# Splitting the weights of a hybrid decoder layer into high and low parts: one operation per pair of K tiles, with three weight buffers

## The chip, the cores and the metric

The kernel runs on one core of a Trainium2 chip. A core has a matrix engine (PE, with its weight loads shown apart as PEld), a vector engine (DVE), a scalar engine (ACT), a fourth engine that this kernel does not use (POOL), and DMA queues that the engines issue; nearly all loads of this kernel are issued by SyncE (SP). The metric is the device time of one execution in microseconds; lower is better. The profile is of one execution of the kernel, taken apart from the timed ones.

## The reference

One decoder layer over 256 tokens of 4096 channels, in float32. The inputs are normalised, projected once to 12,288 columns, mixed in three branches, gated, normalised by branch, projected back, added to the residual and normalised again:

```python
h = rmsnorm(x, ln_g)
proj = h @ w_in                                   # 4096 x 12288
p_x, p_gate, q, k, v, a_gate, s_u, s_gate = jnp.split(proj, _SPLIT_OFFSETS, axis=-1)
y_pool = pool_mixer(p_x, w_pool, pool_scale)
y_attn = stick_breaking_attention(q, k, v)        # reshaped to 16 heads
y_ssm  = s5_mixer(s_u, ..., w_glu, b_glu)         # ends in a GLU: h @ w_glu
...                                               # per branch: rmsnorm, times silu(gate)
out = rmsnorm(x + concat(branches) @ w_out, final_g)
```

## The kernel before

**Precision.** A float32 product is made of three matmuls in a reduced format (fp32r): each operand is split into a high part, which is a rounded copy, and a low part, the operand less that copy, and the products high x high, high x low and low x high are summed in PSUM. ScalarE makes the high part (a copy with rounding), VectorE the low part (a subtraction that reads the weights and the high part).

**The stream.** All weights come as one stream of 528 steps (`N_SUB`). A step is a pair of K tiles: one weight tile `w` of 128 partitions x 2 x 512 float32, 512 KB, loaded by one DMA on SP's queue. Steps 0 to 399 are the input projection (24 units of 512 columns with 16 steps each) and four shorter GLU units of 4 steps; steps 400 to 527 are the output projection, eight "out" units of 16 steps. In the loop (L860 to L921) step i first issues the load of step i + 4 (`LOAD_AHEAD`), then splits the weights of step i + 2 (`SPLIT_AHEAD`), then issues the matmuls of step i, and then pumps a share of the side work of the three branches (scans, attention, gates, transposes).

**Forms of a step.** `mm_chan` (L241 to L247) has the weights as the stationary operand and makes 24 matmuls of 256 columns; `mm_tok` (L234 to L239) streams the weights and makes 12 matmuls of 512 columns. In each out unit the steps 2, 5, 7, 9 and 11 (`SEVEN`) are made by the seven-product scheme of Strassen and Winograd on the four 128 x 256 blocks of the weight pair, 21 matmuls of 256 columns (`mm_seven`, L169 to L185). Such a step needs three raw blocks in high and low parts (`split_seven`, L158) and four sums of blocks, also in high and low parts (`sums_seven`, L147: the differences `t7` by VectorE, then a high part of 128 x 1024 by ScalarE and a low part of 128 x 1024 by VectorE). They are joined at the unit's end (`join_seven`, L187).

**What sets the order.** SP's queue is issued in the order in which the code is written. The order on the other engines is made by a scheduler when the program is built, which knows the operations and their dependences; each engine then runs its queue strictly in that order. A tile from a pool with n buffers waits until the last reader of the tile n allocations earlier is done. So a load of `w` waits for the low part of the pair whose buffer it takes, and a high part waits for the matmuls that read the buffer that it takes.

**Names and lines.** `load_first` L125 (step 0, loaded as two halves with the first pieces of x between them), `load` L135, `hi_lo` L140, `split` L210 (high part at L228, low part through the helper at L82), `split_x` (the activations, ACT at L94 and DVE at L91), `constants` L717 (four small loads at the start of unit 1, i.e. step 16; three pass through one staging tile `raw`), `square_x` (sums of squares of x, one piece `xsq` of 512 KB at eight of the steps from 16 on), `load_out` L759 (residual `xr` and norm weights `fg` at step 7 of each out unit). In the last four steps the matmuls of the second token half are held back to the tail (L927 to L947), so their split weights stay in tiles of their own (`held8`, `held4`).

Of the kernel before, what the change touches and what calls it, by code (L numbers as in the profile page):

```python
# [23 lines left out]
NU = 512  # L24
# [5 lines left out]
LOAD_AHEAD = 4  # L30
SPLIT_AHEAD = 2
HELD = 4
# [20 lines left out]
N_SUB = 24 * 16 + 4 * 4 + 8 * 16  # L53


def body(tc, a, out, ctx):
# [20 lines left out]
    bp = pool("base")  # L77
# [3 lines left out]
    def tt(o, x, y, op):  # L81
        V.tensor_tensor(o, x, y, op)  # L82
# [10 lines left out]
    def act(o, x, f, **kw):  # L93
        S.activation(o, x, f, **kw)  # L94
# [25 lines left out]

# [1 line left out]
    wtiles, htiles = {}, {}  # L122
    held = []

    def load_first():  # L125
        w = wp.tile([P, 2, NU], F32, tag="w", bufs=LOAD_AHEAD, name="w")
        xt = bp.tile([P, 2, L], F32, tag="k4", bufs=6, name="xt")
        for j in range(2):
            nc.sync.dma_start(w[:, j, :], a["ws"][0, :, j, :])
            if j == 0:  # L130
                nc.sync.dma_start(prm, a["prm"])
            nc.sync.dma_start(xt[:, j, :], a["xT"][0, :, j, :])
        wtiles[0], xtiles[0] = w, xt

    def load(i):  # L135
        w = wp.tile([P, 2, NU], F32, tag="w", bufs=LOAD_AHEAD, name="w")
# [10 lines left out]
    def sums_seven(i):  # L147
        w = wtiles[i]
        left, right = w[:, :, 0:L], w[:, :, L:2 * L]
        t = bp.tile([P, 4, L], F32, tag="k4", bufs=6, name="t7")  # L150
        tt(t[:, 0:2, :], right, w[:, 0, :].rearrange("p (c m) -> p c m", c=2), ALU.subtract)
        tt(t[:, 2, :], right[:, 1, :], t[:, 0, :], ALU.subtract)
        tt(t[:, 3, :], left[:, 1, :], t[:, 2, :], ALU.subtract)
        sums = bp.tile([P, 2, 4, L], F32R, tag="k8", bufs=3, name="sums7")
        hi_lo(sums[:, 0], sums[:, 1], t)
        htiles[i] = sums

    def split_seven(i):  # L158
# [8 lines left out]
        htiles[i] = (raw, htiles[i])  # L167

    def mm_seven(i, s, ps, pp):  # L169
        (b11, b2), sums = htiles.pop(i)  # L170
# [4 lines left out]
        for o, stat, mov, begin, end in (  # L175
            (pp[0], xa[:, :, lo_half], [v[:, 0:L] for v in b11], first, last),
            (ps[:, 0, 0:L], xb[:, :, lo_half], [v[:, 0:L] for v in b2], False, False),
            (ps[:, 0, L:2 * L], y[:, 2], [v[:, L:2 * L] for v in b2], False, False),
            (pp[1], y[:, 0], [sums[:, h, 0] for h in range(2)], False, last),
            (pp[3], xa[:, :, hi_half], [sums[:, h, 1] for h in range(2)], first, last),  # L180
            (pp[2], y[:, 1], [sums[:, h, 2] for h in range(2)], False, last),
            (ps[:, 1, 0:L], xb[:, :, hi_half], [sums[:, h, 3] for h in range(2)], False, False),
        ):
            for k, (p, q) in enumerate(((0, 0), (0, 1), (1, 0))):
                T.matmul(o, stat[:, p, :], mov[q], start=begin and k == 0, stop=end and k == 2, skip_group_check=True)  # L185

    def join_seven(pp, xr):  # L187
        e = bp.tile([P, 4, L], F32, tag="k4", bufs=6, name="e7")
        act(e[:, 0, :], pp[0], AF.Copy)
        tt(e[:, 3, :], e[:, 0, :], pp[2], ALU.add)  # L190
        tt(e[:, 1, :], e[:, 3, :], pp[1], ALU.add)
        tt(e[:, 2, :], e[:, 3, :], pp[3], ALU.add)
        tt(e[:, 3, :], e[:, 2, :], pp[1], ALU.add)
        tt(xr, xr, e.rearrange("p (t c) m -> p t (c m)", t=2), ALU.add)
# [15 lines left out]
    def split(i):  # L210
        if seven(i):
            return split_seven(i)
        w = wtiles.pop(i)
        for kk in range(2):
            if i < KT // 2:
                split_x(2 * i + kk)
            h = 2 * (i - N_SUB + HELD) + kk
            if h < 0:
                hi = wp.tile([P, NU], F32R, tag="hi", bufs=5, name="hi")
                lo = wp.tile([P, NU], F32R, tag="lo", bufs=5, name="lo")  # L220
            elif h < 6:
                if h % 2 == 0:
                    held.append(bp.tile([P, 2, 2, NU], F32R, tag="k8", bufs=3, name="held8"))
                hi, lo = held[-1][:, kk, 0, :], held[-1][:, kk, 1, :]
            else:
                held.append(bp.tile([P, 2, NU], F32R, tag="k4", bufs=6, name="held4"))
                hi, lo = held[-1][:, 0, :], held[-1][:, 1, :]
            made = S.activation(hi, w[:, kk, :], AF.Copy)  # L228
            if i == 12:
                state["gate"] = made.ins.name  # L230
            tt(lo, w[:, kk, :], hi.bitcast(F32), ALU.subtract)
            htiles[i, kk] = (hi, lo)

# [14 lines left out]

# [1 line left out]
    state = {}  # L250
# [28 lines left out]

# [1 line left out]
    def log1pexp_parts(z, l):  # L281
# [47 lines left out]

# [1 line left out]
    pool_sums = cp.tile([P, 2, 2], F32, name="pool_sums")  # L331
# [43 lines left out]

# [1 line left out]
    uT = bp.tile([P, 8, L], F32, tag="k8", bufs=3, name="uT")  # L377
# [206 lines left out]

# [1 line left out]
    aout = {}  # L586
# [66 lines left out]

# [1 line left out]
    cur = {}  # L655
# [31 lines left out]

# [1 line left out]
    units = []  # L689
# [351 lines left out]
```

## Time and profile before

| what | value |
|---|---|
| time, median of 3 runs (lowest, highest) | 1558.77 us (1558.5, 1559.57) |
| profiled execution, span from first to last instruction | 1556.4 us |
| the runs' median less that span | 2.4 us |
| mean granted clock of PE | 0.998 |
| data moved by DMA | 308.45 MB, mean 198 GB/s |
| first matmul starts, last one ends | 5.27 us, 1545.4 us |

The profiled execution's time is taken as its span and what lies around it. The page of a profile lists the busy time of each engine, the span in slices, the chain of work that ended last, and the costliest groups of instructions: line, engine, operation, `out<-in` by the program's names with its shape, the count, busy us, mean ns of one, the idle time of the engine just before them, and what ended most of that. Engines other than the bound one have idle time that costs nothing.

### The profile page before, as it was taken

The numbers are of one execution on the slowest core, as the hardware profiler recorded it, in microseconds if no ns is written. First come the engines' busy times: TensorE is split into PE (matmuls) and PEld (weight loads), VectorE is DVE, ScalarE is ACT, GpSimd is POOL, SyncE is SP. The second block draws the span as 40 slices with busy tenths as digits, with TensorE's granted clock in tenths as the row PEclk, the third lists the DMA queues.
The fourth block names the chain that finished last, engine by engine and source line by source line (L and its number), as shares of the span: only waits on it lengthen the run. The fifth ranks groups of instructions, "written<-read, shape, count | busy, mean of one in ns | idle before, by whom it ended". The sixth has DMA issues, their size and how long they took to land.

```text
span 1556.4 us, 25428 instructions
## 1 busy us (share of the span) xinstructions
PE 1538.2 (99%) x9164; PEld 1360.9 (87%) x9164; DVE 1201.6 (77%) x2325; ACT 913.9 (59%) x1637; POOL 0.2 (0%) x4
## 2 busy tenths in 40 slices
PE   8999999999999999999999999999999999999996
PEld 8998788888799989998998889988888888888885
DVE  7579978999898879897556745455678888888886
ACT  7655556666565555565546754456667655555554
POOL 0000000000000000000000000000000000000000
PEclk9999999999999999999999999999999999999999
DMA  8866656566655546554555555545556666666665
GB/s 320 306 214 205 195 162 205 186 206 194 205 188 185 187 156 197 176 175 162 183 186 180 180 185 183 183 159 186 190 178 193 212 220 220 216 214 210 204 222 198
DMA packets 94079, 308.45 MB, mean 198 GB/s; under 512 B 11777, under 2 KB 17665, under 8 KB 93953
## 3 DMA queue, kind: packets, MB, share of 16 engines
q1 hardware_dynamic: 84096, 296.08, 58.2%
q10 hardware_dynamic: 9856, 10.76, 2.3%
q8 instruction: 71, 1.16, 0.3%
q14 instruction: 56, 0.45, 0.1%
HBM read 299.45 MB, written 4.19 MB: 195 GB/s over the span
## 4 chain that ended last, share of the span: by engine, by line
PE 96%; DVE 2%; DMA 1%; ACT 1%; issue 0%; SPq 0%; DVEq 0%; ACTq 0%
PE pm L238 18%; PE pm L237 18%; PE pm L239 18%; PE pm L245 10%; PE pm L247 10%; PE pm L246 10%; PE ps L185 3%; PE pm L185 3%; DVE lo L82 1%; PE ps_y L572 1%; DMA w<-in_ws 1%; PE ps_bu L545 0%; ACT hi L228 0%; PE ps_z L598 0%; PE ps_p L356 0%; PE ps_t L296 0%
## 5 line engine op out<-in xcount | busy, mean ns | idle before, releaser
L82 DVE TENSOR_TENSOR lo<-w,hi 128x512 fp32r<-128x512 f32 (+1 forms) x1048 | 696.9, 678 | 273.1 <-ACT hi L228 266.0
L228 ACT ACTIVATE hi<-w 128x512 fp32r<-128x512 f32 x968 | 604.6, 629 | 503.2 <-PE pm L239 204.4
L238 PE MATMUL pm<-lo,xhl 128*128 128x512 f32 x1232 | 482.4, 392 | 0.0
L239 PE MATMUL pm<-hi,xhl 128*128 128x512 f32 x1232 | 480.8, 390 | 0.0
L237 PE MATMUL pm<-hi,xhl 128*128 128x512 f32 x1232 | 480.6, 390 | 0.0
L245 PE MATMUL pm<-xhl,hi 128*128 128x256 f32 x1280 | 363.8, 284 | 5.3 <-ACT xhl L94 5.3
L246 PE MATMUL pm<-xhl,hi 128*128 128x256 f32 x1280 | 363.5, 284 | 0.0
L247 PE MATMUL pm<-xhl,lo 128*128 128x256 f32 x1280 | 363.4, 284 | 0.0
L238 PEld LDWEIGHTS pm<-lo,xhl 128*128 128x128 f32 x1232 | 231.5, 188 | 48.9 <-issue 2.1
L239 PEld LDWEIGHTS pm<-hi,xhl 128*128 128x128 f32 x1232 | 231.4, 188 | 47.3 <-issue 1.2
L237 PEld LDWEIGHTS pm<-hi,xhl 128*128 128x128 f32 x1232 | 231.5, 188 | 46.9 <-issue 0.4
L245 PEld LDWEIGHTS pm<-xhl,hi 128*128 128x128 f32 x1280 | 246.6, 193 | 7.1 <-ACT xhl L94 5.3
L247 PEld LDWEIGHTS pm<-xhl,lo 128*128 128x128 f32 x1280 | 246.6, 193 | 1.2 <-issue 0.8
L246 PEld LDWEIGHTS pm<-xhl,hi 128*128 128x128 f32 x1280 | 246.6, 193 | 0.8 <-issue 0.4
L91 DVE SCALAR_TENSOR_TENSOR et<-et,pw,tr 128x16 f32<-128x16 f32 (+3 forms) x256 | 55.6, 275 | 2.3 <-ACT tr L94 1.9
L94 ACT ACTIVATE sums<-t 128x1024 fp32r<-128x1024 f32 x40 | 42.3, 1058 | 23.8 <-DVE t L82 23.3
L82 DVE TENSOR_TENSOR sums<-t,sums 128x1024 fp32r<-128x1024 f32 x40 | 48.9, 1223 | 8.8 <-ACT sums L94 8.7
L94 ACT ACTIVATE hi<-w 128x256 fp32r<-128x256 f32 x80 | 40.0, 518 | 22.4 <-PE pm L239 18.9
L185 PE MATMUL ps<-sums,s 128*128 128x256 f32 x240 | 46.5, 283 | 1.1 <-DVE sums L82 1.1
L94 ACT ACTIVATE tr<-et,pw 128x32 f32<-128x32 f32 (+3 forms) x128 | 44.7, 384 | 4.7 <-DVE et L91 2.0
L82 DVE TENSOR_TENSOR t<-w 128x512 f32<-128x512 f32 x40 | 27.6, 690 | 24.3 <-DMA w<-in_ws 24.0
L560 DVE TENSOR_TENSOR_SCAN tb<-rho,ta 128x256 f32<-128x256 f32 x64 | 40.6, 676 | 0.1
(258 smaller groups left out, 1261.3 us busy)
## 6 DMA issues: line engine op xcount, KB each, us to landing
w<-in_ws SPq DMA_DIRECT2D x527, 512.0 KB, 3.5
xsq<-in_xr SPq DMA_DIRECT2D x8, 512.0 KB, 7.2
xr<-in_xr SPq DMA_DIRECT2D x8, 512.0 KB, 4.5
out<-o SPq DMA_DIRECT2D x8, 512.0 KB, 4.0
xt<-in_xT SPq DMA_DIRECT2D x15, 256.0 KB, 6.1
b<-in_bst ACTq DMA_DIRECT2D x16, 192.0 KB, 3.6
u<-uT ACTq DMA_DIRECT2D x96, 32.0 KB, 3.0
fg<-in_fg SPq DMA_DIRECT2D x8, 256.0 KB, 5.9
```

The source lines that it names most:

```text
L82: V.tensor_tensor(o, x, y, op)
L91: V.scalar_tensor_tensor(o, x, s, y, op0, op1)
L94: S.activation(o, x, f, **kw)
L185: T.matmul(o, stat[:, p, :], mov[q], start=begin and k == 0, stop=end and k == 2, skip_group_check=True)
L228: made = S.activation(hi, w[:, kk, :], AF.Copy)
L237: T.matmul(ps[t], stat[:, slot, 0, sl], hi, start=first, stop=False)
L238: T.matmul(ps[t], stat[:, slot, 0, sl], lo, start=False, stop=False)
L239: T.matmul(ps[t], stat[:, slot, 1, sl], hi, start=False, stop=last)
L245: T.matmul(o, hi[:, c], xhl[:, slot, 0, :], start=first and j % 2 == 0, stop=False, skip_group_check=True)
L246: T.matmul(o, hi[:, c], xhl[:, slot, 1, :], start=False, stop=False, skip_group_check=True)
L247: T.matmul(o, lo[:, c], xhl[:, slot, 0, :], start=False, stop=last, skip_group_check=True)
L560: V.tensor_tensor_scan(tb[:, c, :], rho[:, pr:pr + 1].broadcast_to([P, L]), ta[:, c, :], 0.0, ALU.mult, ALU.add)
```

## The change

The high and low parts of a weight pair become one tile each of 2 x 512 columns, made by one operation per engine (L225 and the helper at L82) in place of two of 512. For the sevenfold steps one operation of 768 columns stands in place of one of 256 and one of 512; so that the three raw blocks lie side by side, the roles of the left and right block column are exchanged, and the differences `t7` are four operations of 256 columns in place of one of 512 and two of 256. The pools change: `w` has three buffers in place of four, `hi` and `lo` three pairs each in place of five halves, `fg` one in place of two. `LOAD_AHEAD` stays 4. The activations of a step (`split_x`) are now written ahead of both halves of the weights.

```diff
 def load(i):
-    w = wp.tile([P, 2, NU], F32, tag="w", bufs=LOAD_AHEAD, name="w")
+    w = wp.tile([P, 2, NU], F32, tag="w", bufs=3, name="w")
 def sums_seven(i):
-    left, right = w[:, :, 0:L], w[:, :, L:2 * L]
+    left, right = w[:, :, L:2 * L], w[:, :, 0:L]
-    tt(t[:, 0:2, :], right, w[:, 0, :].rearrange("p (c m) -> p c m", c=2), ALU.subtract)
+    tt(t[:, 0, :], right[:, 0, :], left[:, 0, :], ALU.subtract)
+    tt(t[:, 1, :], right[:, 1, :], right[:, 0, :], ALU.subtract)
 def split_seven(i):
-    w = wtiles.pop(i)
-    raw = []
-    for kk in range(2):
-        n = L if kk == 0 else NU
-        hi = wp.tile([P, NU], F32R, tag="hi", bufs=5, name="hi")
-        lo = wp.tile([P, NU], F32R, tag="lo", bufs=5, name="lo")
-        hi_lo(hi[:, 0:n], lo[:, 0:n], w[:, kk, 0:n])
-        raw.append((hi, lo))
+    w = wtiles.pop(i).rearrange("p k n -> p (k n)")
+    hi = wp.tile([P, 2 * NU], F32R, tag="hi", bufs=3, name="hi")
+    lo = wp.tile([P, 2 * NU], F32R, tag="lo", bufs=3, name="lo")
+    raw = slice(L, 2 * NU)
+    hi_lo(hi[:, raw], lo[:, raw], w[:, raw])
 def mm_seven(i, s, ps, pp):
-    (ps[:, 0, 0:L], xb[:, :, lo_half], [v[:, 0:L] for v in b2], False, False),
-    (ps[:, 0, L:2 * L], y[:, 2], [v[:, L:2 * L] for v in b2], False, False),
+    (ps[:, 0, L:2 * L], xb[:, :, lo_half], b21, False, False),
+    (ps[:, 0, 0:L], y[:, 2], b22, False, False),
...
 def split(i):
-    for kk in range(2):
-        if i < KT // 2:
-            split_x(2 * i + kk)
-        h = 2 * (i - N_SUB + HELD) + kk
-        if h < 0:
-            hi = wp.tile([P, NU], F32R, tag="hi", bufs=5, name="hi")
-            lo = wp.tile([P, NU], F32R, tag="lo", bufs=5, name="lo")
...
-        made = S.activation(hi, w[:, kk, :], AF.Copy)
-        tt(lo, w[:, kk, :], hi.bitcast(F32), ALU.subtract)
+    if i < KT // 2:
+        split_x(2 * i)
+        split_x(2 * i + 1)
+    h = i - N_SUB + HELD
+    if h < 0:
+        hi = wp.tile([P, 2, NU], F32R, tag="hi", bufs=3, name="hi")
+        lo = wp.tile([P, 2, NU], F32R, tag="lo", bufs=3, name="lo")
+    elif h < 3:
+        t = bp.tile([P, 2, 2, NU], F32R, tag="k8", bufs=3, name="held8")
+        hi, lo = t[:, 0], t[:, 1]
+    else:
+        hi = bp.tile([P, 2, NU], F32R, tag="k4", bufs=6, name="held4")
+        lo = bp.tile([P, 2, NU], F32R, tag="k4", bufs=6, name="held4")
+    made = S.activation(hi, w, AF.Copy)
+    tt(lo, w, hi.bitcast(F32), ALU.subtract)
...
 def load_out(n):
-    fg = ep.tile([P, NU], F32, tag="fg", bufs=2, name="fg")
+    fg = ep.tile([P, NU], F32, tag="fg", bufs=1, name="fg")
```

In three places the order of the instructions shows what this does. The first is ScalarE's queue at the start of the program; `hi` are high parts of the weights of the first steps, `xhl` those of the activations. Before:

```order
L69 ACT_TABLE_LOAD
L228 ACTIVATE hi<-w 128x512
L94 ACTIVATE xhl<-xt,prm 128x256
L228 ACTIVATE hi<-w 128x512
L94 ACTIVATE xhl<-xt,prm 128x256 x3
L228 ACTIVATE hi<-w 128x512 x2
L94 ACTIVATE xhl<-xt,prm 128x256 x2
```

And now:

```order
L69 ACT_TABLE_LOAD
L94 ACTIVATE xhl<-xt,prm 128x256
L225 ACTIVATE hi<-w 128x1024
L94 ACTIVATE xhl<-xt,prm 128x256 x3
L225 ACTIVATE hi<-w 128x1024
L94 ACTIVATE xhl<-xt,prm 128x256 x2
```

The high part of the first weights stood ahead of the first activations and covered one half; it now stands behind them and covers both halves.

The second place is ScalarE's queue around the constants (`tneg`, `oneneg`, `maskb` from the staging tile `raw`; `junk` are the squares of a piece of x). A number stands behind each name; before, the tiles w_661, w_699, w_733 and w_784 are those of steps 17, 18, 19 and 20. Before:

```order
L228 ACTIVATE hi_735<-w_661 128x512
L94 ACTIVATE tneg_77<-raw_769 128x128
L228 ACTIVATE hi_739<-w_661 128x512
L228 ACTIVATE hi_786<-w_699 128x512
L94 ACTIVATE oneneg_78<-raw_772 128x128
L228 ACTIVATE hi_790<-w_699 128x512
L94 ACTIVATE maskb_80<-raw_775 128x128
L228 ACTIVATE hi_826<-w_733 128x512
L228 ACTIVATE hi_830<-w_733 128x512
L94 ACTIVATE junk_781,x_sums_86<-xsq_779 128x512 x2
L228 ACTIVATE hi_860<-w_784 128x512
```

And now, where w_635, w_665 and w_712 are the tiles of steps 18, 19 and 20:

```order
L225 ACTIVATE hi_714<-w_635 128x1024
L94 ACTIVATE tneg_77<-raw_697 128x128
L225 ACTIVATE hi_750<-w_665 128x1024
L94 ACTIVATE oneneg_78<-raw_700 128x128
L94 ACTIVATE maskb_80<-raw_703 128x128
L94 ACTIVATE junk_709,x_sums_86<-xsq_707 128x512 x2
L225 ACTIVATE hi_780<-w_712 128x1024
```

The copies that free the staging tile stood between the halves of steps 17 and 18 (`tneg`, `oneneg`) and behind step 18 (`maskb`); they now stand behind the whole pairs of steps 18 and 19. The first two squares stay ahead of step 20.

The third place is VectorE's queue in the fifth out unit, around the sevenfold step 9 (`t7` are its differences of blocks, `sums7` the low parts of its sums; the `lo` behind the first `t7` is that of step 8). Before:

```order
L82 TENSOR_TENSOR t7_15419<-w_15409 128x512
L82 TENSOR_TENSOR lo_15416<-w_15358,hi_15415 128x512
L82 TENSOR_TENSOR lo_15450<-w_15387,hi_15449 128x512
L82 TENSOR_TENSOR t7_15419<-w_15409,t7_15419 128x256
L82 TENSOR_TENSOR lo_15454<-w_15387,hi_15453 128x512
L82 TENSOR_TENSOR t7_15419<-w_15409,t7_15419 128x256
L82 TENSOR_TENSOR lo_15472<-w_15409,hi_15471 128x256
L82 TENSOR_TENSOR lo_15476<-w_15409,hi_15475 128x512
```

And now:

```order
L82 TENSOR_TENSOR t7_13554<-w_13548 128x256 x2
L82 TENSOR_TENSOR lo_13586<-w_13530,hi_13585 128x1024
L82 TENSOR_TENSOR t7_13554<-w_13548,t7_13554 128x256 x2
L82 TENSOR_TENSOR lo_13604<-w_13548,hi_13603 128x768
L82 TENSOR_TENSOR lo_13643<-w_13583,hi_13642 128x1024
```

In both orders the first difference of step 9 stands ahead of the low part of step 8, so that one waits for the load of step 9. What that load waits for has moved: with four buffers it takes the tile of step 5, with three that of step 6.

More of the change, by code (lines that the diff above doesn't have):

```diff
@@ L135, in load @@
     def load(i):
-        w = wp.tile([P, 2, NU], F32, tag="w", bufs=LOAD_AHEAD, name="w")
+        w = wp.tile([P, 2, NU], F32, tag="w", bufs=3, name="w")
         nc.sync.dma_start(w, a["ws"][i])
@@ L158, in split_seven @@
     def split_seven(i):
-        w = wtiles.pop(i)
-        raw = []
-        for kk in range(2):
-            n = L if kk == 0 else NU
-            hi = wp.tile([P, NU], F32R, tag="hi", bufs=5, name="hi")
-            lo = wp.tile([P, NU], F32R, tag="lo", bufs=5, name="lo")
-            hi_lo(hi[:, 0:n], lo[:, 0:n], w[:, kk, 0:n])
-            raw.append((hi, lo))
-        htiles[i] = (raw, htiles[i])
+        w = wtiles.pop(i).rearrange("p k n -> p (k n)")
[3 more added lines that the diff above has]
+        hi_lo(hi[:, raw], lo[:, raw], w[:, raw])
+        htiles[i] = ((hi, lo), htiles[i])
     def mm_seven(i, s, ps, pp):
-        (b11, b2), sums = htiles.pop(i)
+        raw, sums = htiles.pop(i)
+        b11, b22, b21 = ([v[:, j * L:j * L + L] for v in raw] for j in (1, 2, 3))
         xa, xb, y = xhl[:, 2 * s], xhl[:, 2 * s + 1], state["s7"][s]
@@ L175, in mm_seven @@
         for o, stat, mov, begin, end in (
-            (pp[0], xa[:, :, lo_half], [v[:, 0:L] for v in b11], first, last),
-            (ps[:, 0, 0:L], xb[:, :, lo_half], [v[:, 0:L] for v in b2], False, False),
-            (ps[:, 0, L:2 * L], y[:, 2], [v[:, L:2 * L] for v in b2], False, False),
+            (pp[0], xa[:, :, lo_half], b11, first, last),
+            (ps[:, 0, L:2 * L], xb[:, :, lo_half], b21, False, False),
+            (ps[:, 0, 0:L], y[:, 2], b22, False, False),
             (pp[1], y[:, 0], [sums[:, h, 0] for h in range(2)], False, last),
@@ L181, in mm_seven @@
             (pp[2], y[:, 1], [sums[:, h, 2] for h in range(2)], False, last),
-            (ps[:, 1, 0:L], xb[:, :, hi_half], [sums[:, h, 3] for h in range(2)], False, False),
+            (ps[:, 1, L:2 * L], xb[:, :, hi_half], [sums[:, h, 3] for h in range(2)], False, False),
         ):
@@ L188, in join_seven @@
         e = bp.tile([P, 4, L], F32, tag="k4", bufs=6, name="e7")
[L189 to L193, printed above, removed]
+        act(e[:, 1, :], pp[0], AF.Copy)
+        tt(e[:, 2, :], e[:, 1, :], pp[2], ALU.add)
+        tt(e[:, 0, :], e[:, 2, :], pp[1], ALU.add)
+        tt(e[:, 3, :], e[:, 2, :], pp[3], ALU.add)
+        tt(e[:, 2, :], e[:, 3, :], pp[1], ALU.add)
         tt(xr, xr, e.rearrange("p (t c) m -> p t (c m)", t=2), ALU.add)
@@ L213, in split @@
         w = wtiles.pop(i)
-        for kk in range(2):
-            if i < KT // 2:
-                split_x(2 * i + kk)
-            h = 2 * (i - N_SUB + HELD) + kk
-            if h < 0:
-                hi = wp.tile([P, NU], F32R, tag="hi", bufs=5, name="hi")
-                lo = wp.tile([P, NU], F32R, tag="lo", bufs=5, name="lo")
[L221 to L230, printed above, removed]
-            tt(lo, w[:, kk, :], hi.bitcast(F32), ALU.subtract)
-            htiles[i, kk] = (hi, lo)
+        if i < KT // 2:
[12 more added lines that the diff above has]
+        made = S.activation(hi, w, AF.Copy)
+        if i == 12:
+            state["gate"] = made.ins.name
+        tt(lo, w, hi.bitcast(F32), ALU.subtract)
+        for kk in range(2):
+            htiles[i, kk] = (hi[:, kk, :], lo[:, kk, :])
     def mm_tok(ps, stat, slot, hi, lo, first, last, toks=(0, 1)):
```

1 line of the change is left out of this document (removed).

## The prediction

> **What bounds the kernel now.** The page comes first: span, busy shares and the chain of work that ended last.
>
> ```profile
> span 1556.4 us, 25428 instructions
> PE 1538.2 (99%) x9164; PEld 1360.9 (87%) x9164; DVE 1201.6 (77%) x2325; ACT 913.9 (59%) x1637; POOL 0.2 (0%) x4
> PE 96%; DVE 2%; DMA 1%; ACT 1%; issue 0%; SPq 0%; DVEq 0%; ACTq 0%
> ```
>
> TensorE is busy for 99% of the span and is 96% of the chain. A share is an average, so the second view is busy time in stretches of 40 us (columns: stretch, length, then busy us of PE, PEld, DVE, ACT, POOL, granted clock, DMA share, GB/s).
>
> ```profile
> 0.00:40.00 40.00, 34.73 (x268) 34.50 (x269) 29.52 (x59) 29.78 (x58) 0.20 (x4) 1.00 0.89 318
> 400.00:440.00 40.00, 40.00 (x204) 32.18 (x204) 34.53 (x73) 22.55 (x44) 0.00 (x0) 1.00 0.59 188
> 1200.00:1240.00 40.00, 38.91 (x224) 34.21 (x224) 35.57 (x59) 26.94 (x46) 0.00 (x0) 1.00 0.68 217
> 1240.00:1280.00 40.00, 40.00 (x227) 35.12 (x226) 33.97 (x57) 23.40 (x41) 0.00 (x0) 1.00 0.68 218
> 1520.00:1556.00 36.00, 24.59 (x135) 20.39 (x133) 21.72 (x44) 15.54 (x29) 0.00 (x0) 0.92 0.56 209
> ```
>
> PE is full in every stretch but the first, the last, and 1200 to 1240, where 1.09 us are missing. The matmuls are the same in number and size after the change. So a gain can only come from those three places, and a loss from anywhere that a split or a load comes later than PE needs it. The span is 1556.4 us and the median of the runs 1558.77, which leaves 2.4 us outside the span. I add the sum to the median.
>
> **What the larger operations save, and why I cost it at nothing.** The groups of the page give the durations:
>
> ```profile
> L82 DVE TENSOR_TENSOR lo<-w,hi 128x512 fp32r<-128x512 f32 (+1 forms) x1048 | 696.9, 678 | 273.1 <-ACT hi L228 266.0
> L228 ACT ACTIVATE hi<-w 128x512 fp32r<-128x512 f32 x968 | 604.6, 629 | 503.2 <-PE pm L239 204.4
> L94 ACT ACTIVATE sums<-t 128x1024 fp32r<-128x1024 f32 x40 | 42.3, 1058 | 23.8 <-DVE t L82 23.3
> L82 DVE TENSOR_TENSOR sums<-t,sums 128x1024 fp32r<-128x1024 f32 x40 | 48.9, 1223 | 8.8 <-ACT sums L94 8.7
> ```
>
> A pair's low part is now two operations of 678 ns; the row of 128x1024 has the same kind of work in 1223, so 133 ns are saved for each of the 484 pairs of the row of high parts (968), 64 us of VectorE. On ScalarE two of 629 become one of 1058, 200 ns and 97 us. The idle columns say that this is not on the path: VectorE waits 266 us for ScalarE's high parts, and ScalarE's high parts wait mostly for a matmul to give a buffer back. Both are paced by PE. [...] The price of the larger operation is latency: its consumer needs the first half only, and gets it when the whole pair is done. That is paid wherever PE has no lead.
>
> **Term 1, the start.** The timeline of the first 11 us (start, us, engine, line, operation, and the idle time before it with its releaser):
>
> ```profile
> 3.51 0.63 ACT L228 ACTIVATE hi<-w 128x512 fp32r<-128x512 f32 x1 [1.50 <-DMA w<-in_ws]
> 4.17 0.69 DVE L82 TENSOR_TENSOR lo<-w,hi 128x512 fp32r<-128x512 f32 x1 [3.07 <-ACT hi L228]
> 4.71 0.51 ACT L94 ACTIVATE xhl<-xt,prm 128x256 fp32r<-128x256 f32 x1 [0.57 <-DMA xt<-in_xT]
> ...
> 5.27 0.58 PE L245 MATMUL pm<-xhl,hi 128*128 128x256 f32 x1 [5.27 <-ACT xhl L94]
> ...
> 5.59 0.63 ACT L228 ACTIVATE hi<-w 128x512 fp32r<-128x512 f32 x1 [0.37 <-DMA w<-in_ws]
> ...
> 6.17 0.41 PE L247 MATMUL pm<-xhl,lo 128*128 128x256 f32 x1
> 6.38 0.41 PE L245 MATMUL pm<-xhl,hi 128*128 128x256 f32 x1
> ...
> 10.44 0.35 PE L246 MATMUL pm<-xhl,hi 128*128 128x256 f32 x1
> 10.63 0.28 PE L247 MATMUL pm<-xhl,lo 128*128 128x256 f32 x1
> 10.75 0.28 PE L245 MATMUL pm<-xhl,hi 128*128 128x256 f32 x1
> ```
>
> Before, half 0 is split at 3.51, before half 1 has landed (5.59), and PE starts at 5.27. After, one high part needs both halves: 5.59 + 1.06 = 6.65. The low part takes 1.22 more and ends at 7.9; as here, where PE starts some 0.05 to 0.3 behind its operand, I put the first matmul with a low part (L247, third in order) at 8.15. It was at 6.17: **+2.0 us**. The other steps of the opening have PE behind, not ahead, so nothing takes that back. The bounds come from the clock: matmuls start 0.21 apart up to 10.44 and 0.12 apart from 10.63 on. If the clock opens at the same moment, the delayed work is that of the slow period: from 8.15 on some 11 matmuls fit instead of 20, 9 or 10 x 0.12 = +1.1. If it opens only 5.3 us after 8.15 (the time from the first matmul to the doubling here), some 20 matmuls are missing by then, x 0.12 = +2.4. If it opens as long after the third matmul as here, at 12.6, the whole delay stands, +2.0; I take that, since the gap of 1.2 us ahead of the third matmul leaves little for the time before it to count. [...] I give the rule an even chance within the forecast; both its times lie within the range, one on either side of the bound of 0.2%.
>
> **Term 2, the constants at step 16.** One staging tile serves three small loads in turn, each freed by a ScalarE copy (L723). ScalarE runs its queue in order, and the order of the change puts whole-pair high parts between those copies.
>
> ```profile
> 59.32 0.63 ACT L94 ACTIVATE junk<-xsq 128x512 bf16<-128x512 f32 x1 [0.35 <-DMA xsq<-in_xr]
> ...
> 60.73 1.15 ACT L228 ACTIVATE hi<-w 128x512 fp32r<-128x512 f32 x2
> 61.40 1.29 DVE L82 TENSOR_TENSOR lo<-w,hi 128x512 fp32r<-128x512 f32 x2 [1.71 <-ACT hi L228]
> ```
>
> ```profile
> raw<-in_cst SPq DMA_DIRECT2D x3, 64.0 KB, 2.0
> ```
>
> Now with three pair buffers, counted from the end of PE's step 15, when the buffer for pair 18 comes free: high part of 18 to 1.06, copy tneg, second load issued 1.6, landed 3.6; high part of 19 waits for step 16 (24 matmuls x 0.12 = 2.88), to 3.94; oneneg, third load 4.3 to 6.3; maskb 6.6; the first xsq, behind that load on SP's queue, lands at 8.2 (59.3 above less the 3.5 us since its issue shows the same 3.5); two squares to 9.7; high part of 20 to 10.75, low part 1.22, 12.0. PE needs it at 4 x 2.88 + 0.24 = 11.76. **+0.4** after rounding up for the waits; the cover here was about 2.8 us and is gone. Ends: 0, and 2.5 if the small loads wait behind weight tiles. The next pairs win lead again, as each needs only 2.3 of 2.88 us.
>
> **Term 3, the projection and the branches.** A high part may start when step i-3 is done, two steps of at least 2.7 us ahead of its use, and needs 1.06 + 1.22 = 2.3. VectorE's side work lies between, as before, and the summed work falls. Weight loads are issued one step later than with four buffers:
>
> ```profile
> ACT hi L228 <- DMA w<-in_ws: 4.0, 6, 1.5
> ```
>
> Over 968 high parts, loads were waited for six times, mostly at the start. **0**, ends 0 and +2.
>
> **Term 4, the first out unit.** The one gap inside:
>
> ```profile
> 1226.24 1.22 DVE L82 TENSOR_TENSOR sums<-t,sums 128x1024 fp32r<-128x1024 f32 x1
> 1227.52 0.50 PE L185 MATMUL ps<-sums,s 128*128 128x256 f32 x2 [1.09 <-DVE sums L82]
> ```
>
> Here VectorE is the bound, loaded by side work and by the sums of step 9. It gets some 0.13 us per pair and loses 0.05 or so per sevenfold step, since the sums' differences are now four operations of 256 (419 ns, and 335 apart back to back) where one of 512 (690) and two of 256 stood. By the new order the sums of step 7 come about 1.2 late and those of step 9 then fit: the wait moves, net **+0.1**, ends -1.1 (gone) and +2.
>
> **Term 5, out units 1 to 7.** With three buffers the load of step 9 waits for the low part of step 6; the differences of step 9 stand ahead of the low part of step 8 in VectorE's queue and wait for that load.
>
> ```profile
> w<-in_ws SPq DMA_DIRECT2D x527, 512.0 KB, 3.5
> w<-in_ws SPq DMA_DIRECT2D x109, 512.0 KB, 3.9
> 1311.01 1.22 DVE L82 TENSOR_TENSOR sums<-t,sums 128x1024 fp32r<-128x1024 f32 x1
> ...
> 1312.74 0.28 PE L185 MATMUL ps<-sums,s 128*128 128x256 f32 x1
> ```
>
> The cycle is landing + two differences (0.67) + the low part (1.22) + issue 0.1, thus landing + 2.0; PE takes 12 x 0.227 = 2.72 for a plain step and 21 x 0.12 = 2.52 for a sevenfold one, 5.24. With the 3.5 us of the whole run (first row; 109 of these units alone give 3.9, second row) the cycle is 5.5, a loss of 0.26 in each of three cycles per unit, 0.8 out of a lead of some 2.9 (5.24 less 2.3) that steps 12 to 1 win back. I take 3.5 and not 3.9, since three buffers leave fewer loads in flight at once. The thinnest lead before is that of the last two rows: sums done at 1312.23, wanted at 1312.74. **0**; the other end is the first rival.
>
> **Term 6, the tail.** The last held pair is one operation too:
>
> ```profile
> 1536.57 1.22 DVE L82 TENSOR_TENSOR xr<-xr,e 128x1024 f32<-128x1024 f32 x1
> ```
>
> VectorE works without a break to 1537.8 and PE is close behind the held low parts. A whole pair gives its first half 0.6 later: **+0.5**, ends 0 and 0.9.
>
> **The sum:** 2.0 + 0.4 + 0 + 0.1 + 0 + 0.5 = 3.0, so 1558.77 + 3.0 = **1561.8 us**, +0.19%.
>
> **The rivals.** *Slower, by the load chain of term 5.* If loads land in 5.0 rather than 3.5 us, that is behind one other transfer (318 GB/s at a share of 0.89 make 357 GB/s, so 524 KB take 1.5), the cycle is 7.0, 1.76 over PE's 5.24; three per unit lose 5.3, the lead of 2.9 covers part of it, and 2.4 per unit stay, 17 in seven: 1579. It decides from a landing of 5.24 - 2.0 + 2.9/3 = 4.2 us. For it: the median of 3.9 in this stretch, and xr and fg on the same queue. Chance 0.2, most of it with partial loss, between 1564 and 1579. *Absorbed:* the clock opens on time and the constants and the tail keep their cover: +1.1 and a little less from term 4, 1559 to 1560. Chance 0.16. *Faster:* VectorE binds more than the gap shows, and its 64 us buy back the 1.09 and the small waits in PE's spacing in the out units; with a start of +1.1 that would need 4 us elsewhere to pass 0.2%: 1555. Nothing in the full stretches shows them. Chance 0.04. *That the change doesn't do what it says* is excluded by the order of the instructions: one operation per engine and pair stands there.
>
> **How the numbers follow.** The forecast has 0.6. 0.2% is 3.1 us, about what a measurement of this kernel can tell from no change, and the forecast of +3.0 lies on that bound, so its chance is halved: 0.3 same and 0.3 slower. With absorbed (0.16, same) and the load chain (0.2, nearly all slower): faster 0.04, same 0.47, slower 0.49. The range runs from 1559.3 (start +1.1 and little else, term 4 regained) to 1569, which takes in constants +2.5, term 3 +2, and half of the load chain.
>
> **What would show it.** [...] PE gaps that end with VectorE's low parts at steps 6, 8 and 10 of each out unit would mean the first rival; PE idle in mid-program released by ScalarE's high parts would refute term 3; a PE start still near 5.3 would refute term 1.

## The result, and the profile after

The changed kernel takes 1567.11 us, the median of four runs between 1564.11 and 1570.34. The kernel before took 1559.17 beside it (1558.5 to 1559.75). The ratio is 1.0052 with a 95% interval of 1.0036 to 1.0069: slower, by some 8 us, where the forecast was 3.0 and the range reached 1569. The runs also spread five times as far as those of before. The traced run is the fastest of the four (1564.1 us, span 1561.4), so the trace shows 5.0 of the 8 us.

The page of the changed kernel, its span, busy shares and chain:

```profile
span 1561.4 us, 23859 instructions
PE 1538.0 (99%) x9164; PEld 1360.5 (87%) x9164; DVE 1158.1 (74%) x1837; ACT 827.7 (53%) x1109; POOL 0.2 (0%) x4
PE 90%; DMA 4%; DVE 4%; ACT 1%; issue 1%; SPq 0%; DVEq 0%; ACTq 0%
```

VectorE has 43.5 us less to do and ScalarE 86, and PE, which sets the time, is busy as long as before (1538.0 against 1538.2). The span grows by idle time of PE alone. The chain passes through DMA for 4% and VectorE for 4%, where it had 1% and 2%; these shares are far more than 5 us, so they say where to look and not what was lost. Busy time by stretch (columns as before):

```profile
0.00:40.00 40.00, 32.74 (x259) 32.45 (x260) 27.55 (x44) 26.94 (x43) 0.20 (x4) 1.00 0.85 296
80.00:120.00 40.00, 38.37 (x259) 35.48 (x258) 26.66 (x72) 19.40 (x31) 0.00 (x0) 1.00 0.69 230
400.00:440.00 40.00, 40.00 (x191) 31.52 (x190) 34.76 (x64) 18.50 (x25) 0.00 (x0) 1.00 0.61 198
1200.00:1240.00 40.00, 39.12 (x227) 34.41 (x226) 35.00 (x53) 25.24 (x31) 0.00 (x0) 1.00 0.63 209
1240.00:1280.00 40.00, 40.00 (x227) 35.20 (x226) 32.72 (x43) 21.73 (x25) 0.00 (x0) 1.00 0.60 207
1480.00:1520.00 40.00, 39.07 (x216) 33.99 (x216) 33.38 (x46) 20.27 (x25) 0.00 (x0) 1.00 0.64 217
```

PE loses 2.0 us more in the first stretch, 1.6 in that from 80 to 120, and 0.9 in one of the out units; from 120 to 1200 every stretch is full (those not shown too). The groups and one row of the waits:

```profile
L82 DVE TENSOR_TENSOR lo<-w,hi 128x1024 fp32r<-128x1024 f32 (+1 forms) x524 | 628.7, 1201 | 304.5 <-ACT hi L225 300.6
L225 ACT ACTIVATE hi<-w 128x1024 fp32r<-128x1024 f32 x484 | 511.8, 1058 | 513.6 <-PE pm L237 239.0
```

```profile
ACT hi L225 <- DMA w<-in_ws: 34.3, 31, 2.4
```

The pair operations cost what the rows of before promised (1058 ns by ScalarE; the two forms of VectorE together 1201). The engines save less than the 64 and 97 us that the prediction worked out, since the two halves of before overlapped where they ran back to back: 1.29 us for both in the prediction's row at 61.40, not twice 678 ns. What is saved became idle time, and high parts now wait for weight loads for 34.3 us, where it was 4.0.

A view by step says where PE falls behind: the start of the first matmul of a step, less the same step's start in the trace of before, and so the growth over each part of the program. The second column is a later trace of the same kernel (run e1, 1565.5 us), the third what the prediction had:

```
part                                  after   e1     predicted
1 start (to step 8)                   +1.1   +2.4    +2.0
2 constants (steps 8 to 22)           +0.5   +0.7    +0.4
3 projection and branches (to 400)    +1.6   +1.5     0
4 first out unit (to step 416)        -0.3   -0.4    +0.1
5 out units 1 to 7 (to step 526)      +1.4   +2.2     0
6 tail                                +0.6   +0.5    +0.5
sum                                   +4.9   +6.9    +3.0
```

**Term 1**, the start (start, us, engine, line, operation):

```profile
4.67 0.51 ACT L94 ACTIVATE xhl<-xt,prm 128x256 fp32r<-128x256 f32 x1 [2.66 <-DMA xt<-in_xT]
5.68 1.06 ACT L225 ACTIVATE hi<-w 128x1024 fp32r<-128x1024 f32 x1 [0.50 <-DMA w<-in_ws]
...
6.76 1.23 DVE L82 TENSOR_TENSOR lo<-w,hi 128x1024 fp32r<-128x1024 f32 x1 [1.07 <-ACT hi L225]
6.79 0.58 PE L243 MATMUL pm<-xhl,hi 128*128 128x256 f32 x1 [6.79 <-ACT hi L225]
...
8.05 0.58 PE L245 MATMUL pm<-xhl,lo 128*128 128x256 f32 x1 [0.47 <-DVE lo L82]
...
10.35 0.37 PE L243 MATMUL pm<-xhl,hi 128*128 128x256 f32 x1
10.56 0.28 PE L244 MATMUL pm<-xhl,hi 128*128 128x256 f32 x1
10.68 0.28 PE L245 MATMUL pm<-xhl,lo 128*128 128x256 f32 x1
```

The third matmul comes at 8.05, as worked out (8.15). But matmuls start 0.21 us apart only up to 10.56 and 0.12 apart from there, at about the same moment as before (10.63), though PE starts 1.5 us later; so the delay shrinks to 1.1. In the trace of e1 PE starts 0.2 earlier and its rate doubles 3.1 us later, at 13.71, and the delay is 2.4:

```profile
13.33 0.41 PE L243 MATMUL pm<-xhl,hi 128*128 128x256 f32 x1
13.55 0.32 PE L244 MATMUL pm<-xhl,hi 128*128 128x256 f32 x1
13.71 0.28 PE L245 MATMUL pm<-xhl,lo 128*128 128x256 f32 x1
```

So the moment does not follow PE's start; over thirteen traces it comes 3.4 to 7.1 us after it (last section). It is to such a clock, one that opens without regard to PE's start, that the prediction gave an even chance within its forecast; the two traces lie at its bounds of +1.1 and +2.4.

**Term 3, missed**, is a wait of PE for the tile of step 32. Its PSUM buffer is freed by `uT`, which needs the norm of x: two tiles `rb`, each through PE (`ps_r`), in one place used in turn. The timeline after:

```profile
95.51 0.29 DVE L86 TENSOR_SCALAR rb<-ones,rtok 128x128 f32<-128x128 f32 x1
...
98.41 0.38 PE L275 MATMUL ps_r<-ident,rb 128*128 128x128 f32 x2
98.83 0.29 DVE L86 TENSOR_SCALAR rb<-ones,rtok 128x128 f32<-128x128 f32 x1 [0.55 <-PE ps_r L275]
...
101.38 0.38 PE L275 MATMUL ps_r<-ident,rb 128*128 128x128 f32 x2
...
103.87 0.47 PE L235 MATMUL pm<-hi,xhl 128*128 128x512 f32 x1 [1.63 <-DVE uT L82]
```

And before, the same two passes through PE:

```profile
92.94 0.38 PE L277 MATMUL ps_r<-ident,rb 128*128 128x128 f32 x2
...
95.91 0.38 PE L277 MATMUL ps_r<-ident,rb 128*128 128x128 f32 x2
```

The chain runs 5.5 us later than before, more than PE's own delay of 1.6 there, and its end passes PE's need. Some 4 of the 5.5 us it has from the squares (their rows are under e7); the passes themselves are as long as before.

**Term 5**, the gap of 0.93 us at step 9 of the seventh out unit:

```profile
1481.11 1.22 DVE L82 TENSOR_TENSOR lo<-w,hi 128x1024 fp32r<-128x1024 f32 x1
...
1482.36 0.33 SPq L136 DMA_DIRECT2D w<-in_ws  x1
...
1485.99 0.76 DVE L82 TENSOR_TENSOR t<-w 128x256 f32<-128x256 f32 x2 [0.86 <-DMA w<-in_ws]
1486.67 1.22 DVE L82 TENSOR_TENSOR sums<-t,sums 128x1024 fp32r<-128x1024 f32 x1
...
1487.94 0.50 PE L183 MATMUL ps<-sums,s 128*128 128x256 f32 x2 [0.93 <-DVE sums L82]
```

One reads the first rival here: the low part of step 8 frees the tile (1482.33), the load of step 11 is issued at once and lands 3.6 us later, its differences `t` head VectorE's queue and wait for it, and what stands behind them is late. Only, what stands behind are the sums of step 9, not the low part of step 10.

### The profile page after: what moved, and what is told of

The parts are those of the page before. It is cut to its first block, busy times and chain, and to the rows that moved or that the text cites. A ratio compares the mean times of both kernels' runs of the same rounds, so it can differ in the third digit from the quotient of the medians.

```text
span 1561.4 us, 23859 instructions
## 1 busy us (share of the span) xinstructions
PE 1538.0 (99%) x9164; PEld 1360.5 (87%) x9164; DVE 1158.1 (74%) x1837; ACT 827.7 (53%) x1109; POOL 0.2 (0%) x4
## 4 chain that ended last, share of the span: by engine, by line
PE 90%; DMA 4%; DVE 4%; ACT 1%; issue 1%; SPq 0%; DVEq 0%; ACTq 0%
PE pm L236 17%; PE pm L235 17%; PE pm L237 17%; PE pm L245 10%; PE pm L243 10%; PE pm L244 10%; DMA w<-in_ws 4%; PE ps L183 3%; PE pm L183 2%; DVE lo L82 2%; PE ps_y L570 1%; DVE t L82 1%; ACT hi L225 1%; PE ps_bu L543 0%; PE ps_z L596 0%
## 5 line engine op out<-in xcount | busy, mean ns | idle before, releaser
L82 DVE TENSOR_TENSOR lo<-w,hi 128x1024 fp32r<-128x1024 f32 (+1 forms) x524 | 628.7, 1201 | 304.5 <-ACT hi L225 300.6
L225 ACT ACTIVATE hi<-w 128x1024 fp32r<-128x1024 f32 x484 | 511.8, 1058 | 513.6 <-PE pm L237 239.0
L94 ACT ACTIVATE hi<-w 128x768 fp32r<-128x768 f32 x40 | 33.8, 846 | 52.9 <-PE pm L237 45.9
L94 ACT ACTIVATE sums<-t 128x1024 fp32r<-128x1024 f32 x40 | 42.3, 1058 | 28.5 <-DVE t L82 28.3
L82 DVE TENSOR_TENSOR sums<-t,sums 128x1024 fp32r<-128x1024 f32 x40 | 48.9, 1222 | 5.5 <-ACT sums L94 5.4
L82 DVE TENSOR_TENSOR t<-w 128x256 f32<-128x256 f32 x80 | 30.5, 421 | 27.0 <-DMA w<-in_ws 26.9
```

Of the source, the lines that this page charges most:

```text
L225: made = S.activation(hi, w, AF.Copy)
```

## The experiments

Two theories. **Latency**: a whole pair gives its first half later, and PE, which has no lead in a few places, waits there; the buffers are innocent. **Buffers**: three weight tiles make each load wait a step longer, and the out units lose. All medians below are of five or more runs but that of e5 (four), with the kernel before beside them at medians of 1557.8 to 1558.1 us. In e2, e3, e4, e6 and e8 the traced run is the fastest of its series, so their traces show less than the medians; losses by step are against the trace of before, a run of 1558.77 us.

**e1, the changed kernel again.**

> The changed kernel as it is, once more, for a second trace and its spread. Its four runs were 1564.1 to 1570.3 us and the traced one is the fastest. If three weight buffers make the out units sensitive to load times, the runs spread over 4 to 6 us again, and a trace of a longer run shows more PE gaps at sevenfold steps between 1240 and 1540 us, with the start (first matmul 6.8) and step 32 (some 2 us lost) unchanged. If the spread is of some other origin, the extra time lies outside the span or in the first 400 us.

1565.51 us (1564.03 to 1566.93), ratio 1.005 (1.0038 to 1.0063). The second column of the table above is its trace. It took the median time of its series, 6.7 us over the traced run of before, and the six parts account for all of that. Start and out units both differ from the first trace, by 1.2 and 0.8 us, so the spread has at least two sources, not one.

**e2, three buffers alone.**

> The kernel before with three weight buffers in place of four and nothing else changed. If the loss comes from the latency of whole-pair operations: within 1 us of before (1559 to 1560 us), spread as before. If three buffers alone make the load chain of the out units bind: +3 to +8 us, with PE gaps at sevenfold steps and a wider spread.

```diff
 def load_first():
-        w = wp.tile([P, 2, NU], F32, tag="w", bufs=LOAD_AHEAD, name="w")
+        w = wp.tile([P, 2, NU], F32, tag="w", bufs=3, name="w")
...
 def load(i):
-        w = wp.tile([P, 2, NU], F32, tag="w", bufs=LOAD_AHEAD, name="w")
+        w = wp.tile([P, 2, NU], F32, tag="w", bufs=3, name="w")
```

1570.85 us (1568.06 to 1571.77), ratio 1.0081 (1.0068 to 1.0093): 13 us slower than before, and slower than the whole change. One stretch over the out units 1 to 6, in the kernel before and in e2:

```profile
1240.00:1500.00 260.00, 260.00 (x1441) 227.41 (x1440) 218.92 (x359) 150.34 (x256) 0.00 (x0) 1.00 0.66 215
```

```profile
1240.00:1500.00 260.00, 256.37 (x1420) 223.60 (x1419) 214.66 (x353) 146.08 (x251) 0.00 (x0) 1.00 0.64 211
```

By step e2 loses 0.4 us up to step 34, 0.3 more to step 400, 4.2 in the first out unit and 5.3 in the others. Three buffers cost time on their own, where the sevenfold steps are, and hardly elsewhere. Of the 4.2 us some 1.5 are not waiting, an estimate: after a wait of 3.45 us at step 408 the granted clock is 0.50 for 3.4 us, in which PE works 2.94, and at the full clock that work would take half as long:

```profile
1225.40:1228.80 3.40, 2.94 (x12) 2.85 (x13) 3.40 (x7) 1.06 (x1) 0.00 (x0) 0.50 1.04 390
```

From 1240 to 1500 the granted clock is 1.00. With the same three buffers the changed kernel loses far less, -0.3 and 1.4 or 2.2 us; what in it makes up for the rest was not tried.

**e3, half operations on pair tiles.**

> The changed kernel with its pair tiles and three weight buffers, but each high and low part made by two operations again (512 + 512, in sevenfold steps 256 + 512), and the activations between the halves as before. Latency theory: the start (1.1 us), the wait at step 32 (2 us) and the tail (0.9 us) come back, 4 us under the changed kernel, about 1563. Buffer theory: out units lose as much or more, since VectorE has 64 us more to do: 1566 to 1570 with the start at 5.3 us.

```diff
-        raw = slice(L, 2 * NU)
-        hi_lo(hi[:, raw], lo[:, raw], w[:, raw])
+        for raw in (slice(L, NU), slice(NU, 2 * NU)):
+            hi_lo(hi[:, raw], lo[:, raw], w[:, raw])
...
-        if i < KT // 2:
-            split_x(2 * i)
-            split_x(2 * i + 1)
...
-        made = S.activation(hi, w, AF.Copy)
...
-        tt(lo, w, hi.bitcast(F32), ALU.subtract)
         for kk in range(2):
+            if i < KT // 2:
+                split_x(2 * i + kk)
+            made = S.activation(hi[:, kk, :], w[:, kk, :], AF.Copy)
...
+            tt(lo[:, kk, :], w[:, kk, :], hi[:, kk, :].bitcast(F32), ALU.subtract)
```

1562.7 us (1559.28 to 1563.97, eight runs), ratio 1.0027 (1.0016 to 1.0037), 2.8 under e1. In its trace, of the run of 1559.28, start, constants and step 32 lose nothing (0.0 at step 34), and it is 1.6 us ahead of before at step 400; the out units 1 to 7 then lose 2.7. Both theories hold there, each in its place; where the median loses another 3.4 us no trace shows.

**e4, the first pair in halves.**

> The changed kernel with only the pair of step 0 split in halves. First matmul at 5.3 in place of 6.8 us, step 1 starts 1.1 us earlier than in the changed kernel, and nothing else moves: 1.1 us under the changed kernel. If the later wait at step 32 absorbs it, the span gains less than 0.5.

1565.7 us (1564.93 to 1568.78), ratio 1.0054: nothing gained. PE starts at 5.44, but the wait has moved to step 1, as these rows show:

```profile
9.68 1.06 ACT L228 ACTIVATE hi<-w 128x1024 fp32r<-128x1024 f32 x1 [1.94 <-DMA w<-in_ws]
...
10.79 0.39 PE L246 MATMUL pm<-xhl,hi 128*128 128x256 f32 x1 [0.60 <-ACT hi L228]
...
12.05 0.39 PE L248 MATMUL pm<-xhl,lo 128*128 128x256 f32 x1 [0.76 <-DVE lo L82]
```

**e5, a fourth weight buffer in the out units.**

> The changed kernel with a fourth weight buffer for the out units only (there is no room for it before step 400); to make room the scratch tile of the row sums moves to another pool. Buffer theory: the losses at sevenfold steps between 1240 and 1540 us go, the spread of the runs falls to some 2 us, and the median falls by 2 to 5 us against the changed kernel, to 1561 to 1563. Latency theory alone: the same as the changed kernel, 1565 to 1567.

```diff
-        w = wp.tile([P, 2, NU], F32, tag="w", bufs=3, name="w")
+        if i > 404 and i % 4 == 1:
+            w = ep.tile([P, 2, NU], F32, tag="w4", bufs=1, name="w")
+        else:
+            w = wp.tile([P, 2, NU], F32, tag="w", bufs=3, name="w")
...
-            t = qp.tile([P, 3, P], F32, tag="t", bufs=1, name="ts")
+            t = bp.tile([P, 3, P], F32, tag="k4", bufs=6, name="ts")
```

1574.83 us (1574.5 to 1575.53), ratio 1.0108: a miss by the median, the opposite of what was expected. By step, it loses 9.1 us at one place, step 405: the load into the new buffer was not issued before 1221.29, 14 us behind the load ahead of it, and all loads behind it on SP's queue stood still. Its memory had belonged to the pool of the tile `ao`, whose last transposes PE starts at 1220.98. PE waits 4.2 us for the weights, and then its granted clock stands at 0.50 for 10.2 us:

```profile
1221.29 0.33 SPq L139 DMA_DIRECT2D w<-in_ws  x1
...
1225.49 0.50 PE L186 MATMUL ps<-hi,xhl 128*128 128x256 f32 x1 [4.23 <-ACT hi L94]
```

```profile
1225.60:1235.80 10.20, 8.42 (x29) 7.06 (x30) 9.41 (x16) 5.91 (x6) 0.00 (x0) 0.50 0.74 264
106.00:109.40 3.40, 3.40 (x10) 2.61 (x9) 3.26 (x17) 0.00 (x0) 0.00 (x0) 0.51 0.35 85
```

The 8.42 us of work at half rate would take half as long at the full one, so some 4.2 of the 9.1 us are the clock, an estimate. The second row is behind step 32: after the wait of 1.80 us there the granted clock is 0.51 for 3.4 us, which is, by the same estimate, 1.7 of the 2.2 us by which e5 comes later to step 400 than e1. After step 416 it loses nothing, where the changed kernel lost 1.4 and 2.2, and its runs lie within 1.0 us.

**e6, both undone.**

> Both undone at once: two operations per pair (as in e3) and a fourth weight buffer in the out units (as in e5); the pair tiles and the mirrored blocks stay. If latency and buffers are the whole loss, the time is that of before or less, 1556 to 1559, with a narrow spread. If the mirrored blocks with their fourth difference cost something of their own, 1560 or more with VectorE ending last at sevenfold steps.

1565.19 us (1564.87 to 1565.92), ratio 1.0046. The same 9.2 us are lost at step 405, and the mean granted clock of the runs is 0.994 or 0.995, like the 0.993 and 0.994 of e5; everything else is ahead of before: -1.5 us at step 400, and no loss from step 416 on.

**e7, staging tiles apart.**

> The changed kernel with the three constants and the two row tiles of the norm in places of their own instead of one staging tile used in turn. If the waits at steps 20 to 22 (0.5 us) and 32 (1.9 us) come from that tile, both go: 2 to 2.4 us under the changed kernel at step 34. If they come from the whole-pair operations ahead in the queues of ScalarE and VectorE alone, the loss at step 32 stays within 0.5 us.

```diff
+        rbs = bp.tile([P, 2, P], F32, tag="k4", bufs=6, name="rb")
...
-            rb = cp.tile([P, P], F32, tag="rb", bufs=1, name="rb")
+            rb = rbs[:, t, :]
...
+        raws = bp.tile([P, 8, P], F32, tag="k4", bufs=6, name="raws")
...
-            raw = cp.tile([P, P], F32, name="raw", tag="rb", bufs=1)
+            raw = raws[:, i, :]
```

1563.0 us (1561.42 to 1566.51), ratio 1.0032 (1.0019 to 1.0044), 2.5 under e1. At steps 20 to 22 the loss is gone, and so is the wait at step 32:

```profile
93.44 0.48 DVE L86 TENSOR_SCALAR rb<-ones,rtok 128x128 f32<-128x128 f32 x2
...
93.78 0.71 PE L276 MATMUL ps_r<-ident,rb 128*128 128x128 f32 x4 [0.28 <-DVE rb L86]
94.97 0.42 DVE L277 COPY rrow<-ps_r 128x256 f32<-128x256 f32 x1
```

The two passes through PE are one, and `rrow` is there at 95.4 in place of 102.4. It came in part at PE's expense, which waits 0.3 here: the delay grows from 1.2 to 2.0, and is 2.0 at step 34, against 3.5 in the changed kernel. That is 1.5 us, less than the 2 to 2.4 expected. At step 400 it is 2.5 against 3.2, so half of that gain is left there. The edit gives two sorts of tiles their own places, the constants and `rb`. That it is `rb` that counts at step 32 shows in the row behind the squares, here in e7, in the changed kernel and in the kernel before:

```profile
90.76 0.17 DVE L269 TENSOR_REDUCE s_x<-x_sums 128x2 f32<-128x16 f32 x1 [1.25 <-ACT junk L94]
91.08 0.17 DVE L269 TENSOR_REDUCE s_x<-x_sums 128x2 f32<-128x16 f32 x1 [0.36 <-ACT junk L94]
86.97 0.17 DVE L271 TENSOR_REDUCE s_x<-x_sums 128x2 f32<-128x16 f32 x1
```

Of the 7.0 us by which `rrow` comes earlier, 0.3 are there behind the squares, 1.8 come from the small operations from there to `rb`, and 5.0 from the passes.

**e8, sums written one step later** (`SUMS_AHEAD = 0`).

> The changed kernel with the sums of a sevenfold step written one step later, so that its differences no longer stand ahead of the low part of the pair before, waiting for a load. If the chain low part, load, differences, low part is what makes three buffers too few, the out units lose 1 to 3 us less than in the changed kernel. If the sums then come too late themselves, PE waits for them at most sevenfold steps and the kernel is slower by 5 us or more.

1565.56 us (1562.46 to 1568.28), ratio 1.0049 (1.0035 to 1.0062). The trace is as the buffer theory has it, a loss of 0.1 us from step 416 to 526 in place of 1.4 and 2.2; the median and the spread are those of the changed kernel. One trace, of the fastest run of a kernel that spreads by 6 us, does not settle it.

**e9, half operations and a fourth buffer from step 417 on.**

> As e6 (two operations per pair, a fourth weight buffer), but the fourth buffer is used from the second out unit on (step 417). In e6 PE lost 9.2 us once, at step 405, where that buffer waited for the memory of the pool before it, and nothing after. Without that: 1565.2 - 9.2 = 1556.0 us, 2 under before, with PE gaps in the first out unit at most. If three buffers in the first out unit cost what they cost the kernel before with three (5 us), 1561.

1557.35 us (1555.64 to 1557.87, eleven runs), ratio 0.9992 (0.9983 to 1.0001). The 9.2 us at step 405 are gone, and the granted clock is 1.00 from 1200 to 1240, where e5 had 0.87. The first out unit, still with three buffers, loses nothing in sum (-1.0 us at step 400, -1.4 at step 416), and the others nothing at all:

```profile
1240.00:1500.00 260.00, 260.00 (x1442) 227.60 (x1441) 221.03 (x390) 145.86 (x256) 0.00 (x0) 1.00 0.64 214
```

**e10, the first four pairs in halves, staging apart.**

> As e7 (staging apart), with the pairs of steps 0 to 3 split in halves. In e4, with step 0 alone in halves, the wait moved to step 1. If the start is a matter of the whole-pair latency of the first few pairs, the delay at step 8 is within 0.2 of before, in place of 1.2, and the median is 1 to 1.3 us under e7 (1561.8). If weight loads set it, the delay at step 8 stays over 0.8.

1562.18 us (1559.64 to 1564.53, eleven runs), ratio 1.0023 (1.0014 to 1.0032). At step 8 it is 0.3 us ahead of before, at step 34 too: the front of the program is repaired. In the traced run 1.9 us are then lost in out units 1 to 7, with three buffers, as in e1. The median gained 0.8 over e7, less than the 1.5 at step 8.

**e11, halves in the projection and the tail, whole pairs in the out units, fourth buffer from step 417 on.**

> Two operations per pair in the input projection and the tail, one per pair in the out units, the fourth weight buffer from step 417 on. By the two theories together, each where it holds: the front as in e3 (1.5 us ahead of before at step 400), the out units without loss, 1556 to 1557. If whole-pair operations cost something in the out units even with four buffers, 1 us or more over e9.

1556.9 us (1555.82 to 1559.2, eleven runs), ratio 0.9991 (0.9982 to 1.0001). The out units lose nothing with whole pairs either (-1.7 us at step 416, -1.8 at step 526), and VectorE has 5 us less to do there than in e9:

```profile
1240.00:1500.00 260.00, 260.00 (x1442) 227.41 (x1441) 215.71 (x293) 134.58 (x159) 0.00 (x0) 1.00 0.65 215
```

e9 and e11 are the best of all; against the changed kernel they gain some 8 us, against the kernel before about 1, which their intervals do not tell from none.

## Why the prediction came out as it did

**What held.** That nothing is to be gained: 130 us of work were taken from two engines, PE's own time stayed within 0.2 us, and the full stretches from 120 to 1200 stayed full. That the loss ahead of step 400 is latency at places without lead: e3, with the same tiles and half operations, has none of it there. Terms 2 and 6 came out at 0.5 and 0.6, against 0.4 and 0.5; term 4 at -0.3, against +0.1.

**Term 1** was taken between its bounds, at +2.0; it measured 1.1 and 2.4, the one bound and the other, with PE's rate doubled at 10.56 and at 13.71; it doubled at 12.6, the forecast's own case, in neither. Its side claim, that PE is behind in the other steps of the opening, holds for the changed kernel, but only because pair 0 is late: in e4 PE waits for pair 1, whose low part is done at 12.0. With four pairs in halves the start costs nothing (e10).

**Term 3** is the step that failed first: "VectorE's side work lies between, as before". One chain of that side work was not as before. It begins with the squares that term 2 delays, runs through the single tile `rb` and twice through PE's queue, and ends at the PSUM buffer of step 32. The 2 us are within the end that was named, but the cover of that chain was not looked up. e7 takes 1.6 of the 2.4 us that terms 2 and 3 cost by step 34 away by giving the tiles places of their own, though the squares come as late; so it took the shared tile to turn a delay of ScalarE into one of PE.

**Term 5** was put at 0, with the load chain as the first rival at 0.2, from a landing of 4.2 us on. The rival happened with loads that land in 3.7 (the median of 110 in the trace after; 4.1 in that of e1). That the third buffer less is the cause, e2 and e5 show from both sides: three buffers alone lose 5.3 us in the units 1 to 7, a fourth buffer loses none. What was wrong is which operation comes late, and the point from which that decides. The prediction set the lead of 2.9 us of a low part against the cycle; but the sums stand behind the same differences, and the thinnest lead that it quoted itself, 0.5 us, was that of sums. With that lead in place of 2.9, its own formula decides at 5.24 - 2.0 + 0.5/3 = 3.4 us, under every median seen. That is an argument, and it gives the point and not the size: at 3.7 the formula would then charge 0.9 us per unit, some 6 in seven, where 1.4 were lost, and at 4.1 more than twice that, where 2.2 were.

**The median** lies 5.3 us above the forecast: in the trace of e1, whose run is the median of its series, 3.9 us over the forecast are accounted for: 0.4 in term 1, 0.3 in term 2, 1.5 in term 3 and 2.2 in term 5, less 0.5 in term 4. Where the rest went in the first series is open: its runs of 1566.7 to 1570.3 left no trace. Their granted clock is 0.997, like that of the traced run, and 3.4 us at half clock would lower it by 0.001, so it was not that. The kernels with four buffers (e5, e6, e9, e11) spread by 1.0 to 3.4 us, those with three by 2.9 to 6.2, so loads in the out units are the likely part; that is a comparison of spreads, not a trace. In e2 and e4 some slower runs have a granted clock of 0.995 or 0.996, where their traced runs have 0.997, so part of their spread may be time at a lower clock; those runs left no trace. The range held because its upper end had in it what came, term 3 at +2 and part of the load chain.

## What to carry to other kernels

Where one engine is full, as PE is here at 99%, larger operations elsewhere bought nothing (130 us less work, some 8 us more time) and cost the wait for their last element; look for it where the full engine has no lead, at the start (1.1 and 2.4 us here), around a tile that is used in turn (1.6 us, as e7 shows), and at the end (0.6 and 0.5 us). A buffer fewer was paid, with 5.3 us in the units 1 to 7 of e2, where a queue runs in order: what stands behind the first reader of a load inherits its wait, so the lead to compare with is the thinnest of all that stand behind it (0.5 us here, not 2.9). And if the buffer is wanted for room in one phase only, it can be had back in the others, if its memory is free when it is first loaded: e9 loses nothing in the out units, e5 lost 9.1 us at step 405. Look at the granted clock behind a long wait: part of the loss may be there, in e5 some 4.2 of those 9.1 us by the estimate above.

## What the runs showed of the hardware

PE's rate doubled between 3.4 and 7.1 us after the first matmul, over thirteen traces of this kernel, its variants and the kernel before: matmuls of 256 columns start 0.21 us apart and then 0.12, from 8.84 us on in e4 with a start at 5.44, and from 13.71 in e1 with a start at 6.58. In the changed kernel it was from 10.56 on, with a start at 6.79. That accounts for the 1.2 us of term 1 between the two traces of the changed kernel: in the 3.15 us from 10.56 to 13.71 e1 starts 15 matmuls in place of 26, and 11 x 0.12 less the 0.2 of the earlier start are 1.1 us, an estimate.

In mid-program the granted clock stood at 0.50 or 0.51 for 3.4 us (e2 from 1225.4, e5 from 106.0) and for 10.2 us (e5 from 1225.6). In the traces of before and of the changed kernel the column of the granted clock has 1.00 from the start, also where matmuls still start 0.21 us apart, until behind the last matmul (1549.9 and 1553.3 us); so the doubling at the start is read from the matmuls, not from that column.

A wait in mid-program cost more than its length in e2 and e5: behind it PE worked at half the granted clock, for 3.4 us behind the wait of 3.45 in e2 and behind that of 1.80 in e5 at step 32, and for 10.2 us behind that of 4.23 in e5 at step 405. Behind the waits at step 32 of 1.63 us in the changed kernel and of 1.6 in e1 it did not: the granted clock there is 1.00 from 80 to 120 us. What sets these waits apart is not shown.
